# A bidirectional Hyena and gated-MLP block on one core: the second half's pairs in another order, and the DFT jobs spread over the first half of the output projection

## The chip, the cores and the metric

The kernel runs on one core of a Trainium2 chip. The metric is device time in microseconds (us) for one execution.

## What is computed

The block works on x of 2048 tokens by 1024 channels in float32. One input projection to 7168 channels feeds two branches, whose outputs go through one output projection. Cut to what matters here:

```python
proj = rms_norm(x, pre_norm_w) @ w_in
hy_in, hy_gate, sg_u, sg_v, sg_gate = split(proj, [3*D, 4*D, 5*D, 6*D])
x0, x1, v = split(short_conv_centred(hy_in, conv_w, conv_b), 3)
k = hyena_filter(...)                                   # a 4096-long filter per channel
y_a = x0 * long_conv_bidir(v * x1, k, skip) * silu(hy_gate)          # branch A, by DFT
vn = layer_norm_per_head(sg_v)
mixed = einsum('hpq,bnqhd->bnphd', sgu_w, vn) + sgu_b                # 128x128 per head
y_b = sg_u * mixed * silu(sg_gate)                                   # branch B
out = x + rms_norm(concat([y_a, y_b]) @ w_out, post_norm_w)
```

## The kernel before

**Pairs.** Each large product is done by a two by two scheme with seven products in place of eight, over *pairs* of 128-channel blocks. `self.order` is a list of 72 pairs (half, kind, index, and two weight blocks). Half 0 and half 1 are the two halves of the tokens. Kinds: U (x1 and v, whose product goes into the long convolution), G (x0 and branch A's gate), V (two heads of the gating values), B (branch B's gate and sg_u), O (two output blocks). For O the numbers 0 and 1 name not tokens but input channels: O(0) multiplies branch A's channels, O(1) branch B's, and the two partial sums are added. A pair is 84 matmuls of 128x512: seven units of four blocks, each in three matmuls over high and low parts (L304, L305, L306). A stream of pairs sets the order: products 0 to 4 of a pair, then products 5 and 6 behind product 0 of the next.

**Factors.** The moving operands are seven tiles `x`, one for each unit. When half or channels change they are loaded again: `load_x` (L554) loads them and splits them into high and low parts (L558, L559). At the change to `"w0"` (`turn`) the next pair's weights may not be loaded before all background jobs are through, since they come from Y, which the jobs write. The weights of a pair (`wraw`, `ws`, `wu`) are prepared a pair ahead (L606 to L637); for the second half most come back from DRAM (L631).

**Taking results.** A class for each kind (`TakeG`, `TakeV`, `TakeB`, `TakeO`) reads the banks in four calls, c11, c22, c21, c12, the last two in the next pair. V starts `v_job`: for each head transposes (L980), statistics (L984, L985), square root (L987), scaling (L992), mixing matmuls (L997) and the last step on VectorE (L1000); for half 1 the result goes to DRAM as VM (L969). B of half 1 loads it as `vm` (L174), multiplies (L1005) and writes Y. The first O stage writes partial sums to PT (L236, L243); the second loads them (`o_load`), and `o_job` (L1129 to L1134) does the post-norm.

**Background jobs.** DFT work runs beside the pairs as generators. `background(jobs, rate)` sets how many start at a tick; a pair has 3.5 ticks. 32 forward jobs (`fft_job`, two channel halves of 16 jobs): load, DFT matmul (L1070), complex product with the filter on VectorE (L1073, L1077), second DFT matmul (L1082), write BY. 32 inverse jobs (`inv_job`): load BY, inverse DFT matmul (L1108), transpose (L1114), times XG from the G pairs (L1115), write Y (L1116). An inverse job needs all forward jobs of its channel half and the XG of its channels.

**Order.** A scheduler places the instructions of each engine; each engine then works in order, SP (which issues most transfers) too. Buffers are rings: all tiles made by `wide` share four in this stage (`nw_`), those by `f` share six (`nf`), `ws` has three. A tile taken from a ring waits until the oldest is free.

Of the kernel before, what the change touches and what calls it, by code (L numbers as in the profile page):

```python
# [125 lines left out]
class TakeU(Take):  # L126
# [4 lines left out]
    def c22(self, C, u3):  # L131
        self.rv = self.b.wide([128, 18, 64], "rv")
        self.b.add(self.rv[:, 9:17].rearrange("q j p -> q (j p)"), C, u3)
# [83 lines left out]
class TakeO(Take):  # L217
# [5 lines left out]
    def c22(self, C, u3):  # L223
        self.y[1] = self.b.wide([128, 1024], "y1")
        self.b.add(self.y[1][:, 512:], C, u3)
        if self.h:
            self.part = [self.b.o_load(2 * self.c + 1 - n) for n in range(2)][::-1]

    def c21(self, B):
        y = self.y[1][:, :512]  # L230
        if self.h:
            self.nc.vector.tensor_tensor(y, B, self.part[1][:, :512], op=ALU.add)
            self.b.go(self.b.o_job(2 * self.c + 1, self.y[1], self.part[1], 512))
        else:
            self.nc.scalar.copy(y, B)
            self.nc.sync.dma_start(self.b.PT[2 * self.c + 1], self.y[1])  # L236

    def c12(self, C, u2):
        self.b.add(self.y[0][:, 512:], C, u2)
        if self.h:  # L240
            self.b.go(self.b.o_job(2 * self.c, self.y[0], self.part[0], 0))
        else:
            self.nc.sync.dma_start(self.b.PT[2 * self.c], self.y[0])  # L243


class Body:
# [77 lines left out]
    def build(self):  # L324
        with ExitStack() as st:
            self.pp = st.enter_context(self.pool("pp", space=PSUM))
            self.dp = st.enter_context(self.pool("dp", space=DRAM))
            self.cp = st.enter_context(self.pool("cp"))
            dram = lambda n, s, dt=F32: self.dp.tile(s, dt, name=n)
            self.AU = dram("AU", [256, NJ, D])  # L330
            self.AK = dram("AK", [256, NJ, D])
            self.KF = dram("KF", [2, 32, 128, 512])
            self.BY = dram("BY", [256, NJ, D])
            self.XG = dram("XG", [NJ, 128, 8, 128])
            self.UG = dram("UG", [8, 128, D])
            self.VM = dram("VM", [8, 128, 8, 128])
            self.U0 = dram("U0", [8, 128, D])
            self.Y = dram("Y", [NJ, 128, 16, 128])
            self.WT = dram("WT", [2, 7, 128, 4, 512])
            self.PT = dram("PT", [NJ, 128, D])  # L340
            self.RB = dram("RB", [D])
            self.GD = dram("GD", [NJ, 128, 2, 128])
            self.XS = dram("XS", [7, 128, 4, 512])
            self.load_consts()
            self.xp = st.enter_context(self.pool("xp"))
            U = lambda h: [(h, "U", c, 8 + c, 16 + c) for c in range(8)]
            G = lambda h: [(h, "G", c, c, 24 + c) for c in range(8)]
            B = lambda h: [(h, "B", c, 48 + c, 32 + c) for c in range(8)]
            V = lambda h: [(h, "V", c, 40 + c, 41 + c) for c in range(0, 8, 2)]
            GV = lambda h: [p for n in range(4) for p in G(h)[2 * n:2 * n + 2] + V(h)[n:n + 1]]  # L350
            O = lambda r: [(r, "O", m, 2 * m, 2 * m + 1) for m in range(8)]
            self.order = B(0) + U(0) + GV(0) + U(1) + GV(1) + B(1) + O(0) + O(1)
            self.at, self.prev, self.to_spill = 0, None, []
            self.WS = {p[1:3]: dram(f"WS{p[1]}{p[2]}", [len(SPILL), 128, 2, 512]) for p in self.order[:28]}
            self.seen = set()
            self.wp = st.enter_context(self.pool("wp"))
            with self.pool("rp") as self.rp:
                with self.pool("xs") as xs:
                    self.x_phase(xs)
                with self.pool("sg") as self.fp:  # L360
                    self.nw_ = 3
                    with self.pool("mlp") as ml:
                        self.mlp(ml)
                    with self.pool("k1") as kp:
                        self.background(self.k1_jobs(kp), 1.4)
                        self.run(self.stream(8))
                        self.rest()
                with self.pool("fa") as self.fp:
                    self.nw_, self.nf = 4, 8
                    self.background(self.x_jobs(1), 0.25)  # L370
                    self.run(self.stream(8))
                    self.rest()
                self.nc.sync.dma_start(self.rc, self.RB.rearrange("(c q) -> q c", c=8))
                with self.pool("fd") as self.fp:
                    self.nw_, self.nf, self.nl = 5, 2, 3
                    self.background(self.kfft_jobs(), 0.85)
                    self.run(self.stream(12, 1))
                    self.rest()
                with self.pool("fb") as self.fp:
                    self.nw_, self.nf = 4, 3  # L380
                    self.f1 = self.fp.tile([128, 2, 2, 128], F32R, name="f1")
                    self.nc.gpsimd.dma_start(self.f1, self.i["c_f1"])
                    self.background(self.wo_jobs(), 0.32)
                    self.run(self.stream(8))
                    self.rest()
                with self.pool("fc") as self.fp:
                    self.nw_, self.nf, self.nl = 4, 6, 4
                    self.background(self.fft_jobs(), 1.0)
                    self.run(self.stream(20, "w0"))
                with self.pool("fo") as self.fp:  # L390
                    self.nw_ = 4
                    self.pw = self.fp.tile([128, D], F32, name="pw")
                    self.nc.scalar.dma_start(self.pw, self.i["post_norm_w"].partition_broadcast(128))
                    self.run(self.stream(8, "w1"))
                    self.run(self.stream(8))
                    self.drain()

# [541 lines left out]
    def g_job(self, h, c, r0, sg):  # L939
        nc = self.nc  # L940
        t = self.wide([128, 1024], "t")
        self.conv(t, r0, c, h)
        rc = self.rc[:, c:c + 1]
        if h == 0:
            nc.vector.tensor_scalar(self.gedge[:, c:c + 1], sg[:, 1023:1024], rc, None, op0=ALU.mult)
        yield
        nc.vector.scalar_tensor_tensor(sg, sg, rc, t, op0=ALU.mult, op1=ALU.mult)
        nc.sync.dma_start(self.XG[:, :, c, 64 * h:64 * h + 64].rearrange("j q p -> q j p"), sg.rearrange("q (j p) -> q j p", j=NJ))
        if h:
            e = self.edge[:, c, 0:1]  # L950
            nc.vector.tensor_tensor(e, self.fix[:, c:c + 1], self.gedge[:, c:c + 1], op=ALU.mult)
            nc.sync.dma_start(self.XG[NJ - 1, :, c, 63:64], e)


    def v_job(self, h, hd, vr):
# [82 lines left out]
    def fft_jobs(self):  # L1038
        self.back = [0, 0]
        for g in range(0, 32, 2):  # L1040
            yield self.fft_job(g, 0)
        v = self.inv_jobs()
        for g in range(0, 32, 2):
            yield self.fft_job(g, 1)
            if g > 6:
                yield next(v)
        for _ in range(4):
            yield next(v)
        yield iter(())
        yield from v  # L1050

    def product_tile(self, name):

# [42 lines left out]

    def inv_job(self, j, h):
        nc, g1 = self.nc, self.g1
        assert self.back[h] == 32
        cs = slice(h * 512, h * 512 + 512)  # L1100
        raw = self.two("raw")
        nc.sync.dma_start(raw, self.BY[:, j, cs].rearrange("(d r) c -> r d c", d=2))
        yield
        xg = self.product_tile("xg")
        nc.sync.dma_start(xg.rearrange("q (c p) -> q c p", c=4), self.XG[j, :, 4 * h:4 * h + 4])
        ps = self.bank("b")
        for d in range(2):
            nc.tensor.matmul(ps, g1[:, d], raw[:, d], start=d == 0, stop=d == 1)  # L1108
        y = self.f("y")
        nc.scalar.copy(y, ps)  # L1110
        yield
        ps = self.bank("a")
        for q in range(4):
            nc.tensor.transpose(ps[:, q * 128:q * 128 + 128], y[:, q * 128:q * 128 + 128], self.ident)  # L1114
        nc.vector.tensor_tensor(xg, ps, xg, op=ALU.mult)  # L1115
        nc.sync.dma_start(self.Y[j, :, 4 * h:4 * h + 4], xg.rearrange("q (c p) -> q c p", c=4))  # L1116
# [53 lines left out]
```

## Time and profile before

| what | us |
|---|---|
| median of 3 runs | 2086.94 |
| lowest, highest | 2083.53, 2091.46 |
| the profiled execution | 2081.43 |
| its span, first to last instruction | 2079.6 |
| TensorE busy in it | 1907.2 |
| VectorE busy | 1347.8 |
| ScalarE, GpSimd busy | 855.0, 446.3 |

Busy time is the union of an engine's instructions. PE is TensorE's matmuls, PEld its weight loads, DVE is VectorE, ACT ScalarE, POOL GpSimd, SP the engine that issues transfers. A 128x512 DFT matmul in float32 makes two records in the trace and one row in the order below. TensorE can stand as busy while it gains little: a matmul's end is modelled, so short waits hide in the matmuls themselves. For that reason the time per matmul slot is used beside the busy share. The mean granted clock of TensorE was 0.975.

### The profile page before, as it was taken

The numbers are of one execution on the slowest core, as the hardware profiler recorded it, in microseconds if no ns is written. First come the engines' busy times: TensorE is split into PE (matmuls) and PEld (weight loads), VectorE is DVE, ScalarE is ACT, GpSimd is POOL, SyncE is SP. The second block draws the span as 40 slices with busy tenths as digits, with TensorE's granted clock in tenths as the row PEclk, the third lists the DMA queues.
The fourth block names the chain that finished last, engine by engine and source line by source line (L and its number), as shares of the span: only waits on it lengthen the run. The fifth ranks groups of instructions, "written<-read, shape, count | busy, mean of one in ns | idle before, by whom it ended". The sixth has DMA issues, their size and how long they took to land. (4 is left out here: it accounts for less than half of the span.)

```text
span 2079.6 us, 23943 instructions
## 1 busy us (share of the span) xinstructions
PE 1907.2 (92%) x7832; PEld 1419.1 (68%) x7832; DVE 1347.8 (65%) x2070; ACT 855.0 (41%) x1538; POOL 446.3 (21%) x392
## 2 busy tenths in 40 slices
PE   4689999999999999888999999989999999999997
PEld 3465666777777766666777666656677777887776
DVE  6767878787655545655544888887773226436876
ACT  6344444565434443534444223322322224335443
POOL 3431322233222121111111101101011112323331
PEclk9899999999999999999999999989999999999999
DMA  8388777786779796897786888878978888536563
GB/s 265 110 265 268 238 261 253 227 274 230 247 258 297 259 315 208 327 274 236 256 276 194 294 271 265 282 237 274 302 244 307 282 269 282 194 102 243 192 212 132
DMA packets 330203, 515.89 MB, mean 248 GB/s; under 512 B 107451, under 2 KB 177339, under 8 KB 327359
## 3 DMA queue, kind: packets, MB, share of 16 engines
q1 hardware_dynamic: 263328, 439.58, 64.9%
q10 hardware_dynamic: 61856, 69.81, 9.8%
q0 software_dynamic: 4896, 4.98, 1.0%
q8 instruction: 62, 1.02, 0.2%
q14 instruction: 61, 0.50, 0.1%
HBM read 316.10 MB, written 204.48 MB: 250 GB/s over the span
## 5 line engine op out<-in xcount | busy, mean ns | idle before, releaser
L304 PE MATMUL proj<-x,wu 128*128 128x512 f32 x2016 | 834.9, 415 | 36.0 <-ACT sn L648 15.1
L305 PE MATMUL proj<-x,wu 128*128 128x512 f32 x2016 | 808.2, 401 | 10.6 <-DVE wu L637 8.8
L306 PE MATMUL proj<-x,wu 128*128 128x512 f32 x2016 | 806.6, 400 | 1.2 <-DVE x L559 0.6
L304 PEld LDWEIGHTS proj<-x,wu 128*128 128x128 f32 x2016 | 383.6, 190 | 146.2 <-issue 32.8
L637 POOL TENSOR_TENSOR wu<-wraw,wu 128x512 fp32r<-128x512 f32 x172 | 257.3, 1497 | 1038.1 <-ACT wu L635 855.5
L305 PEld LDWEIGHTS proj<-x,wu 128*128 128x128 f32 x2016 | 383.7, 190 | 113.3 <-issue 24.9
L306 PEld LDWEIGHTS proj<-x,wu 128*128 128x128 f32 x2016 | 383.2, 190 | 94.6 <-issue 12.7
L635 ACT CAST wu<-wraw 128x512 fp32r<-128x512 f32 x216 | 133.5, 619 | 281.6 <-PE proj L306 240.3
L637 DVE TENSOR_TENSOR wu<-ws,wu 128x512 fp32r<-128x512 f32 x176 | 129.7, 739 | 156.0 <-ACT wu L635 155.6
L635 ACT CAST wu<-ws 128x512 fp32r<-128x512 f32 x176 | 108.6, 620 | 220.3 <-PE proj L306 160.3
L648 ACT COPY sn<-proj 128x512 f32<-128x512 f32 x216 | 125.6, 581 | 108.4 <-PE proj L306 80.3
L614 POOL TENSOR_TENSOR ws<-wraw 128x512 f32<-128x512 f32 x44 | 79.0, 1795 | 174.5 <-DVE wu L637 111.7
L1073 DVE TENSOR_TENSOR pa<-b,k 64x512 f32<-64x512 f32 x128 | 87.4, 683 | 40.6 <-PE b L1070 29.8
L614 POOL TENSOR_TENSOR ws<-wraw,ws 128x512 f32<-128x512 f32 x44 | 59.5, 1353 | 223.4 <-DVE wu L637 210.1
L1073 DVE TENSOR_TENSOR pb<-b,k 64x512 f32<-64x512 f32 x128 | 88.8, 694 | 1.8
L614 DVE TENSOR_TENSOR ws<-wraw 128x512 f32<-128x512 f32 x44 | 39.6, 901 | 71.3 <-DMA wraw<-in_w_in_dram 39.2
L1082 PE MATMUL b<-pa,tb 128*128 128x512 f32 x128 | 71.7, 645 | 15.1 <-DVE pa L1077 5.5
L1084 ACT COPY ev<-b 128x512 f32<-128x512 f32 x64 | 37.4, 587 | 99.4 <-PE b L1082 88.8
L559 DVE TENSOR_TENSOR x<-x 128x1024 fp32r<-128x1024 f32 x42 | 56.3, 1381 | 19.2 <-ACT x L558 19.2
L1033 PE MATMUL b<-raw,tk 128*128 128x512 f32 x128 | 62.9, 612 | 5.5 <-issue 4.8
L862 PE MATMUL b<-s,ff 128*128 128x512 f32 x128 | 62.2, 603 | 4.4 <-ACT ev L864 2.9
L1070 PE MATMUL b<-raw,tu 128*128 128x512 f32 x128 | 63.2, 604 | 1.7 <-DMA raw<-AU 1.7
(170 smaller groups left out, 2230.5 us busy)
## 6 DMA issues: line engine op xcount, KB each, us to landing
wraw<-in_w_in_dram SPq DMA_DIRECT2D x84, 512.0 KB, 4.9
WSB<-wu SPq DMA_DIRECT2D x32, 512.0 KB, 4.8
dd<-in_c_dec_dram SPq DMA_DIRECT2D x32, 512.0 KB, 5.6
AK<-ev ACTq DMA_DIRECT2D x64, 256.0 KB, 4.5
WSU<-wu SPq DMA_DIRECT2D x32, 512.0 KB, 4.5
WSG<-wu SPq DMA_DIRECT2D x32, 512.0 KB, 5.0
raw<-AK SPq DMA_DIRECT2D x32, 512.0 KB, 6.9
KF<-ev ACTq DMA_DIRECT2D x32, 512.0 KB, 6.0
```

What stands on the lines that cost most here:

```text
L304: t.matmul(ps, sh, mh, start=first, stop=False, **kw)
L305: t.matmul(ps, sl, mh, start=False, stop=False, **kw)
L306: t.matmul(ps, sh, ml, start=False, stop=last, **kw)
L614: eng.tensor_tensor(t, x, y, op=op)
L635: nc.scalar.copy(w[:, 0], src[u])
L637: eng.tensor_tensor(w[:, 1], src[u], w[:, 0].bitcast(F32), op=ALU.subtract)
L648: self.nc.scalar.copy(s, ps)
L862: nc.tensor.matmul(ps, self.ff[:, d], s[d], start=True, stop=True)
L1033: nc.tensor.matmul(ps, tv[:, n], raw[:, n], start=True, stop=True)
L1070: nc.tensor.matmul(u, tv[0][:, n], raw[:, n], start=True, stop=True)
L1073: nc.vector.tensor_tensor(o, uu, kk, op=ALU.mult)
L1082: nc.tensor.matmul(ps, tv[1][:, n], prod[n], start=True, stop=True)
```

## The change

The second half's pairs stand in another order. Before: G and V mixed, then B, then O(0), then O(1). Now: V and B mixed, then G, then O(1), then O(0). The O pairs of branch B, which need no DFT, move into the DFT stage, so that it has 28 pairs where it had 20. The forward jobs start at 0.55 a tick where jobs started at 1.0; after them come two blank ticks, then the inverse jobs at 1.05, where before the inverse jobs of the first channel half were mixed with the forward jobs of the second. Partial sums are written by O(1) and added in O(0). `xg` comes from the `f` ring (six tiles) where it came from the `ws` ring (three).

```diff
@@ TakeO: c22, c21, c12
-        if self.h:
+        if not self.h:
...
@@ build
-            self.order = B(0) + U(0) + GV(0) + U(1) + GV(1) + B(1) + O(0) + O(1)
+            VB = [V(1)[0]]
+            for n in range(4):
+                VB += V(1)[n + 1:n + 2] + B(1)[2 * n:2 * n + 2]
+            self.order = B(0) + U(0) + GV(0) + U(1) + VB + G(1) + O(1) + O(0)
...
-                    self.background(self.fft_jobs(), 1.0)
-                    self.run(self.stream(20, "w0"))
+                    self.background(self.fft_jobs(), 0.55)
+                    self.run(self.stream(20, "w1"))
+                    self.run(self.stream(8, "w0"))
                 with self.pool("fo") as self.fp:
...
-                    self.run(self.stream(8, "w1"))
                     self.run(self.stream(8))
@@ g_job
             nc.sync.dma_start(self.XG[NJ - 1, :, c, 63:64], e)
+            self.gated_c = c + 1
@@ fft_jobs
-        v = self.inv_jobs()
         for g in range(0, 32, 2):
             yield self.fft_job(g, 1)
-            if g > 6:
-                yield next(v)
-        for _ in range(4):
-            yield next(v)
-        yield iter(())
-        yield from v
+        for _ in range(2):
+            yield iter(())
+        self.rate = 1.05
+        yield from self.inv_jobs()
@@ inv_job
-        assert self.back[h] == 32
+        assert self.back[h] == 32 and self.gated_c >= 4 * h + 4
...
-        xg = self.product_tile("xg")
+        xg = self.f("xg")
```

`VB` is V V B B V B B V B B B B. In the changed kernel the lines of the DFT jobs and of the V jobs stand one to four higher: L1070, L1082, L1108 and L1114 are L1071, L1083, L1109 and L1115, and L997 is L1001.

What moves, at three places. First TensorE behind the last mixing matmuls (`b<-sw,vn`) of the half's second V pair, before. `pa,tb` is the second forward DFT matmul, `raw,tu` the first, `raw,g` the inverse one, `ident,y` its transposes, `proj` the pairs' products:

```order
L997 MATMUL b<-sw,vn 128x128 x8
L1082 MATMUL b<-pa,tb 128x512 x2
L1108 MATMUL b<-raw,g_10785 128x512 x2
L1070 MATMUL b<-raw,tu 128x512
L1114 MATMUL a<-ident,y 128x128 x4
L1070 MATMUL b<-raw,tu 128x512
L1082 MATMUL b<-pa,tb 128x512 x2
L1108 MATMUL b<-raw,g_10785 128x512 x2
L1070 MATMUL b<-raw,tu 128x512
L1114 MATMUL a<-ident,y 128x128 x4
L1070 MATMUL b<-raw,tu 128x512
L304 MATMUL proj<-x_6780,wu 128x512
```

And behind those of the third V pair of the half now:

```order
L305 MATMUL proj<-x_6780,wu 128x512
L1001 MATMUL b<-sw,vn 128x128
L306 MATMUL proj<-x_6780,wu 128x512
L1001 MATMUL b<-sw,vn 128x128 x2
L304 MATMUL proj<-x_6859,wu 128x512
L1001 MATMUL b<-sw,vn 128x128
L305 MATMUL proj<-x_6859,wu 128x512
L306 MATMUL proj<-x_6859,wu 128x512
L1083 MATMUL b<-pa,tb 128x512 x2
L1071 MATMUL b<-raw,tu 128x512
L304 MATMUL proj<-x_6859,wu 128x512
L305 MATMUL proj<-x_6859,wu 128x512
```

The mixing matmuls, two jobs' forward matmuls and two inverse jobs stood together; now single mixing matmuls stand between projections, and one forward job's behind them.

Second VectorE at the scaling (`vn`) of the same two V pairs, before (`pa`, `pb` are the complex product):

```order
L652 TENSOR_TENSOR r0_10681<-proj_10806,sn_10801 128x512
L1077 SCALAR_TENSOR_TENSOR pa_10506<-pb_10507,sgn_171,pa_10506 128x512
L1073 TENSOR_TENSOR pa_10572<-b_10570,k_10518 64x512 x2
L1073 TENSOR_TENSOR pb_10573<-b_10570,k_10518 64x512 x2
L1073 TENSOR_TENSOR pa_10581<-b_10579,k_10518 64x512
L1077 SCALAR_TENSOR_TENSOR pa_10572<-pb_10573,sgn_171,pa_10572 128x512
L1073 TENSOR_TENSOR pa_10581<-b_10579,k_10518 64x512
L1073 TENSOR_TENSOR pb_10582<-b_10579,k_10518 64x512 x2
L992 TENSOR_SCALAR vn_10633<-a_10615,mv_10621,rs_10630 128x128
L1077 SCALAR_TENSOR_TENSOR pa_10581<-pb_10582,sgn_171,pa_10581 128x512
L992 TENSOR_SCALAR vn_10633<-a_10615,mv_10621,rs_10630 128x128 x3
L992 TENSOR_SCALAR vn_10663<-a_10645,mv_10651,rs_10660 128x128 x4
```

And now:

```order
L992 RECIPROCAL rs_10181<-rs_10181 128x4
L989 BN_AGGR mv_10202<-bs_10201 128x2 x2
L996 TENSOR_SCALAR vn_10184<-a_10166,mv_10172,rs_10181 128x128 x4
L992 RECIPROCAL rs_10211<-rs_10211 128x4
L655 TENSOR_TENSOR sg_10321<-proj_10308,sn_10103 128x512
L996 TENSOR_SCALAR vn_10214<-a_10196,mv_10202,rs_10211 128x128 x4
L1074 TENSOR_TENSOR pa_10222<-b_10220,k_10131 64x512 x2
L1074 TENSOR_TENSOR pb_10223<-b_10220,k_10131 64x512 x2
L1074 TENSOR_TENSOR pa_10231<-b_10229,k_10131 64x512
L1078 SCALAR_TENSOR_TENSOR pa_10222<-pb_10223,sgn_171,pa_10222 128x512
```

Complex products of forward jobs stood between the statistics and the scaling, and between the two halves of the scaling; now the statistics, the scaling of one head and that of the other follow each other, and the product comes behind.

Third SP where the `vm` of a B pair is loaded, before (the first B pair, behind the last V pair):

```order
L1102 DMA raw_12499<-BY_66 128x2x512
L608 DMA wraw_12477<-in_w_in_dram 128x512
L969 DMA VM_69<-v0_12014 128x1024
L631 DMA wu_12404<-WSB1_92 128x1024
L1116 DMA Y_71<-xg_12290 128x512
L174 DMA vm_12450<-VM_69 128x1024
L969 DMA VM_69<-v1_12093 128x1024
L631 DMA wu_12452<-WSB1_92 128x1024
```

And now (the first B pair, behind the first two V pairs):

```order
L973 DMA VM_69<-v0_9288 128x1024
L964 DMA bi_10161<-in_sgu_b_dram 128x128
L962 DMA sw_10189<-in_sgu_w_dram 128x128
L634 DMA wu_9704<-WSB1_92 128x1024
L174 DMA vm_9685<-VM_69 128x1024
L973 DMA VM_69<-v1_9358 128x1024
L1061 DMA tu_9727<-in_c_tv_dram 128x2x128
L1024 DMA raw_9788<-AU_63 128x2x512
L1064 DMA k_9790<-KF_65 128x2x512
L634 DMA wu_9709<-WSB1_92 128x1024
```

The load of `vm` stood three rows behind the write of a V pair's first head, among inverse jobs' transfers. Now it stands four rows behind such a write, and the loads of the next forward job (`tu`, `raw`, `k`) and of the next pair's last weights (`wu`) stand behind it.

More of the change, by code (lines that the diff above doesn't have):

```diff
@@ L230, in c21 @@
         y = self.y[1][:, :512]
-        if self.h:
+        if not self.h:
             self.nc.vector.tensor_tensor(y, B, self.part[1][:, :512], op=ALU.add)
@@ L239, in c12 @@
         self.b.add(self.y[0][:, 512:], C, u2)
-        if self.h:
+        if not self.h:
             self.b.go(self.b.o_job(2 * self.c, self.y[0], self.part[0], 0))
```

## The prediction

> **What bounds the kernel now.** I read the page's first part, then the stretches of time with each engine's busy time, then TensorE's groups in the stage that changes, then VectorE's groups there.
>
> ```profile
> span 2079.6 us, 23943 instructions
> PE 1907.2 (92%) x7832; PEld 1419.1 (68%) x7832; DVE 1347.8 (65%) x2070; ACT 855.0 (41%) x1538; POOL 446.3 (21%) x392
> ```
>
> TensorE is busy for 92% of the span, so no other engine is the limit; only time in which TensorE stands or crawls can be won. The stretches below are cut at pair boundaries from the start of the DFT stage (columns: length; busy time and instructions of PE, PEld, DVE, ACT, POOL; granted TensorE clock; share and rate of the DMA engines).
>
> ```profile
> 1141.00:1307.70 166.70, 159.18 (x592) 103.68 (x591) 145.20 (x242) 52.01 (x90) 21.79 (x19) 1.00 0.86 278
> 1307.70:1402.40 94.70, 84.63 (x300) 51.94 (x299) 78.66 (x148) 27.03 (x46) 8.43 (x7) 0.93 0.79 256
> 1402.40:1565.40 163.00, 161.53 (x671) 113.49 (x670) 120.08 (x251) 49.00 (x87) 19.73 (x17) 1.00 0.84 275
> 1565.40:1726.40 161.00, 161.00 (x671) 118.68 (x670) 44.37 (x64) 42.71 (x71) 23.05 (x18) 1.00 0.88 283
> 1726.40:1790.10 63.70, 60.32 (x258) 48.50 (x258) 45.10 (x50) 31.27 (x46) 21.28 (x12) 0.97 0.76 270
> 1790.10:1885.30 95.20, 95.20 (x422) 78.86 (x421) 34.25 (x50) 31.50 (x55) 25.87 (x21) 1.00 0.37 121
> 1885.30:1946.50 61.20, 57.69 (x253) 47.14 (x252) 50.42 (x54) 35.18 (x53) 20.85 (x13) 1.00 0.68 250
> 1946.50:2068.50 122.00, 116.21 (x505) 93.95 (x503) 90.38 (x111) 49.15 (x94) 31.91 (x22) 1.00 0.57 185
> 2068.50:2079.60 11.10, 0.00 (x0) 0.00 (x0) 6.02 (x8) 1.44 (x3) 0.00 (x0) 0.70 0.24 94
> ```
>
> The first three are twelve pairs, G and V of the second half with all forward DFT jobs and 11 inverse ones. Then come six B pairs with inverse jobs (PE 161.00 of 161.00 us), the change to branch A's output channels, five pairs of the output projection alone (95.20 of 95.20), the change to branch B's, six pairs with the post-norm, and the tail. Five pairs are 420 projection matmuls, so one takes 95.20/420 = 0.227 us when nothing is in the way. The chain of waits gives the two other slots:
>
> ```profile
> 1721.68 0.44 PE a L1114 x4
> 1722.11 1.72 PE b L1108 x4
> ```
>
> 0.43 us for one record of a 128x512 DFT matmul, 0.11 us for a 128-wide one. What the twelve pairs hold:
>
> ```profile
> L304 PE MATMUL proj<-x,wu 128*128 128x512 f32 x336 | 145.6, 433 | 0.0
> L305 PE MATMUL proj<-x,wu 128*128 128x512 f32 x336 | 139.9, 416 | 0.0
> L306 PE MATMUL proj<-x,wu 128*128 128x512 f32 x337 | 138.3, 411 | 0.0
> L1082 PE MATMUL b<-pa,tb 128*128 128x512 f32 x126 | 70.6, 646 | 15.1 <-DVE pa L1077 5.5 <-issue 4.9 <-DMA tb<-in_c_tv_dram 2.3
> L1070 PE MATMUL b<-raw,tu 128*128 128x512 f32 x128 | 63.2, 604 | 1.7 <-DMA raw<-AU 1.7
> L1108 PE MATMUL b<-raw,g 128*128 128x512 f32 x44 | 22.1, 627 | 0.0
> L997 PE MATMUL b<-sw,vn 128*128 128x128 f32 x128 | 19.7, 287 | 2.1 <-DVE vn L992 1.4 <-DVE pb L1073 0.6
> L980 PE MATMUL a<-ident,v 128*128 128x128 f32 x64 | 9.8, 275 | 0.0
> L1114 PE MATMUL a<-ident,y 128*128 128x128 f32 x44 | 6.7, 275 | 0.0
> L962 PE MATMUL a<-sw,ones 128*128 128x128 f32 x16 | 3.2, 280 | 0.2 <-DVE bi L963 0.2
> ```
>
> That is 1009 x 0.227 + (126 + 128 + 44) x 0.43 + (128 + 64 + 44 + 16) x 0.11 = 229.0 + 128.1 + 27.7 = 384.8 us of work in 424.4 us (1141.0 to 1565.4). So 39.6 us are lost there. The windows show 7.5 + 10.1 + 1.5 = 19.1 us of it as idle and 0.07 x 94.7 = 6.6 us as half clock, 25.7 together; the rest hides in modelled ends (the projection matmuls show 411 to 433 ns). The largest single part stands in the second stretch:
>
> ```profile
> 1388.34 2.05 PE L1082 MATMUL b<-pa,tb 128*128 128x512 f32 x2 [3.59 <-issue]
> 1392.49 2.04 PE L1082 MATMUL b<-pa,tb 128*128 128x512 f32 x2 [2.11 <-DVE pa L1077]
> ```
>
> Here 28 matmuls of mixing and DFT stand in one heap with no projection between them (the first fence of the order, ahead), and TensorE waits 3.6 and 2.1 us inside it, at 2.05 us for two records that take half that elsewhere: half clock.
>
> Why it waits is VectorE, 145.20 + 78.66 + 120.08 = 343.9 of 424.4 us busy, 81%, and more in the first stretch (87%):
>
> ```profile
> L1073 DVE TENSOR_TENSOR pb<-b,k 64x512 f32<-64x512 f32 x128 | 88.8, 694 | 1.8
> L1073 DVE TENSOR_TENSOR pa<-b,k 64x512 f32<-64x512 f32 x128 | 87.4, 683 | 40.6 <-PE b L1070 29.8 <-DMA k<-KF 8.0 <-ACT ev L1084 0.3
> L1077 DVE SCALAR_TENSOR_TENSOR pa<-pb,sgn,pa 128x512 f32<-128x512 f32 x64 | 54.0, 843 | 0.2
> L992 DVE TENSOR_SCALAR vn<-a,mv,rs 128x128 f32<-128x128 f32 x64 | 21.9, 403 | 0.2
> L984 DVE BATCH_NORM_STATS2 bs<-a 128x6 f32<-128x128 f32 x64 | 16.1, 275 | 2.5 <-PE a L980 2.5
> L1000 DVE SCALAR_TENSOR_TENSOR v<-b,nw,bi 128x512 f32<-128x512 f32 x16 | 11.8, 739 | 3.7 <-PE b L997 3.6
> L985 DVE BATCH_NORM_AGGREGATE mv<-bs 128x2 f32<-128x6 f32 x64 | 10.0, 164 | 0.0
> L1115 DVE TENSOR_TENSOR xg<-a,xg 128x512 f32<-128x512 f32 x11 | 7.5, 682 | 17.2 <-PE a L1114 17.2
> ```
>
> The first three rows are the complex product: (88.8 + 87.4 + 54.0)/32 = 7.2 us of VectorE for each forward job. A V pair costs (21.9 + 16.1 + 11.8 + 10.0)/4 = 15.0 us in its four largest groups. At 3.5 forward jobs a pair VectorE needs 25.2 us for them alone, beside 32 to 36 us of TensorE per pair.
>
> **The change, part by part.**
>
> *Same work.* No matmul, vector operation or transfer is added or removed; TensorE's 7832 instructions only move. So the sum is over lost time alone.
>
> *Forward jobs at 0.55 a tick.* A pair has 3.5 ticks, so 1.9 jobs a pair where 3.5 stood, and the 32 jobs with two blank ticks reach 34/0.55 = 62 ticks, 17.7 of the 20 pairs. VectorE's load for them falls to 1.9 x 7.2 = 13.9 us a pair beside 84 x 0.227 + 1.9 x 8 x 0.43 = 25.6 us of TensorE. The heap goes too: the new order has projections among the mixing matmuls and the DFT matmuls behind them (second fence). What a pair without V still loses is bounded below by nothing (the 161.00 of 161.00 row) and above by the first stretch, 7.5/5 = 1.5 us visible, scaled by 39.6/25.7 to 2.3. I take 1.0, nearer to the third stretch, 1.5/5 = 0.3 visible and 0.46 scaled. Eight pairs: 8.0 us. For the five G pairs that now carry one job each, 0.5: 2.5 us; they were full as B pairs, so this is a loss against before.
>
> *V pairs.* The chain of a V pair (transposes, statistics, square root, scaling, mixing matmul, twice per head) has fewer DFT matmuls to hide behind now. Such pairs of the first half, which run beside light DFT work, and the last V pair of the second half:
>
> ```profile
> 600.80:633.30 32.50, 30.51 (x145) 24.00 (x144) 21.28 (x72) 13.05 (x23) 4.88 (x4) 0.95 0.57 183
> 684.10:720.50 36.40, 33.83 (x153) 25.45 (x152) 23.65 (x73) 15.09 (x27) 5.34 (x5) 0.95 0.67 232
> 771.70:805.40 33.70, 30.70 (x146) 23.88 (x145) 20.02 (x69) 12.97 (x23) 5.13 (x4) 0.95 0.44 155
> 857.40:896.20 38.80, 29.46 (x135) 23.72 (x135) 30.21 (x75) 16.69 (x26) 5.21 (x6) 0.87 0.82 290
> 1531.10:1565.40 34.30, 34.14 (x163) 25.70 (x162) 29.79 (x83) 9.26 (x17) 3.88 (x3) 1.00 0.68 219
> ```
>
> Idle plus what the clock took: 2.0 + 1.6 = 3.6; 2.6 + 1.8 = 4.4; 3.0 + 1.7 = 4.7; 9.3 + 5.0 = 14.3; and 0.2 us for the last, which stood among DFT jobs. Those are the bounds of one V pair. The new V pairs resemble the first three, so I take their mean, 4.2: 4 x 4.2 = 16.8 us. The fourth stood at a change of pools; it is the far end of the range.
>
> The Trainium skill, "TensorE: Matmul & The Clock Gate", Part 1 on the HAM clock gate, says that the clock halves only after a whole idle window of about 3.4 us. The trace does not bear that out here: the first of these rows is at 0.95 with 2.0 us of idle in all. By the page's rule the 1.6 to 1.8 us of clock would not be paid in the first three, a V pair would cost 2.5, and the sum would be 6.8 us lower.
>
> *V and B next to each other.* B's `vm` tile now reads VM two pairs after it is written, and takes the buffer of the V tile that writes it. On SP the load of `vm` stands four rows behind the write, with the next forward job's loads behind it.
>
> ```profile
> VM<-v SPq DMA_DIRECT2D x8, 512.0 KB, 3.7
> vm<-VM SPq DMA_DIRECT2D x8, 512.0 KB, 7.1
> ```
>
> Write and read are 3.7 + 7.1 = 10.8 us. Behind the product with `vm` on VectorE wait the adds of the next pair and the next DFT products. Bounds: nothing (it is loaded at the end of a pair and used in the next) and 10.8 us once. The first V and B are the only such tight neighbours, and most is covered by some 7 us of products; I take 1.0.
>
> *Inverse jobs under the output projection.* 32 jobs at 1.05 a tick end after 30.5 ticks, pair 26.4 of 28. In the five undisturbed output pairs VectorE works 34.25/5 = 6.9 us of 19.0; 3.7 inverse jobs add 3.7 x 0.68 = 2.5. TensorE gets 3.7 x (4 x 0.43 + 4 x 0.11) = 8.0 us more work, which leaves the B pairs. Bounds: nothing, as in the B pairs with the same 3.7 jobs, and 5.8/6 = 1.0 us a pair as under the post-norm, 8 us. I take nothing, since the B row holds the same jobs.
>
> *The changes of factors.* Loading and splitting the seven x tiles lost 3.4 + 0.03 x 63.7 = 5.3 us at the first change and 3.5 at the second. Both stay. The first now meets G's convolution and inverse jobs, the last one the inverse transposes, which stand two products (24 x 0.227 = 5.4 us) later than before, but B's last three transfers are gone from SP there. I take no difference; the bounds are 8.8 us either way (all gone, or doubled).
>
> *xg in another ring, the flag, PT:* the xg tile moves from a ring of three to one of six, no instruction more; PT is written in the pairs that wrote it before and read in the last eight. Post-norm and tail stay at 5.8 and 11.1 us. Each is nothing, hidden under the same pairs as before.
>
> Sum: lost before 39.6; after 8.0 + 2.5 + 16.8 + 1.0 = 28.3; gain 11.3 us. The profiled execution took 2081.4 us (span 2079.6 and 1.8 around it), 5.5 below the median of the three runs, 2086.9. So 2070.1 for one like it, and 2075.6 against the median, 0.54% faster. About 0.5% (10.4 us) is what a measurement of this kernel can tell from no change.
>
> **Rivals.**
>
> *The V pairs hide.* If the spread matmuls cover the mixing chains as they did the last V pair (0.2 us), with 0.46 us for the eight and 0.2 for the five others, 0.8 + 3.7 + 1.0 = 5.5 are lost, gain 34: 2053; with V at 1.5, 2058. For it: that row. Against it: it had heaped DFT jobs beside it, the new V pairs have one or two.
>
> *The loss moves to the factor changes and the projection.* Gain of 11.3, but 5 to 9 us come back where inverse jobs now meet the preparation of output weights: 2081 to 2085, no change that can be told. For it: the chain at the first change passes SP and VectorE. Against it: the DMA engines were busy for 0.76 at that change and 0.37 in the projection, so there is room for the jobs' transfers.
>
> *Slower: V pairs in a bare stream.* Two V pairs follow each other at once, with all four `wide` buffers held, and B must take them back. If each V pair costs what the worst of the first half did, 4 x 14.3 + 8.0 + 2.5 + 1.0 = 68.7 us are lost, 29 more than now: 2116. It decides at (39.6 - 11.5)/4 = 7.0 us a V pair; above 9.6 the kernel is slower by over 0.5%. For it: that row had the same buffers to wait for. Against it: three of four stayed under 5.
>
> **How the numbers follow.** Chances: the forecast 0.52 (its own range 2067 to 2082), V pairs hidden 0.14, loss moved 0.24, slower 0.10. The forecast's part below 2076.5 is some 0.6 of it: faster 0.14 + 0.31 = 0.45, slower 0.10, within 0.5% the other 0.45. The range 2058 to 2091 leaves out about half of the hidden case and nearly all of the slower one, and takes in the doubled factor changes (2075.6 + 8.8 = 2084).
>
> **What would show it.** Right: no heap, and the stretch of twelve V and B pairs shorter than 424 us by more than the 31 us of DFT work and 24 us of inverse work that leave it (9 x 8 x 0.43 and 11 x 2.16); the eight output pairs with inverse jobs full; VectorE near 76% in the V and B pairs, (343.9 - 9 x 7.2 - 11 x 0.68)/(424 - 55 - 11). Wrong: `L1001 <- DVE` waits of over 7 us a V pair, granted clock under 0.95 there, or idle time over 10 us at a change of factors.

## The result, and the profile after

The changed kernel takes 2074.3 us in the median of 5 runs (2066.24 to 2080.18); the kernel before, on the same chip, 2085.82 (2082.41 to 2091.46). The ratio is 0.9942, with a 95% interval of 0.992 to 0.9965: some 12 us or 0.58% faster. The forecast was 2075.6. The profiled execution took 2075.84 us, span 2074.1. Three runs that took far longer than the others of their kernel (2251.2 us in the fifth experiment below, 2400.17 us in the second, 6693.6 us of the kernel before) are left out of all times and ratios; the first was the profiled one, so that kernel was profiled again.

The page's busy times, in the form that the prediction shows of before:

```profile
PE 1904.6 (92%) x7832; PEld 1421.4 (69%) x7832; DVE 1341.6 (65%) x2070; ACT 850.1 (41%) x1536; POOL 442.6 (21%) x392
```

TensorE has as many instructions as before (x7832), and its busy time is 2.6 us less. The stretches of time, with the columns as before (length; busy time and instructions of PE, PEld, DVE, ACT, POOL; granted TensorE clock; share and rate of the DMA engines), cut at the new places: twelve pairs from the first V pair's chain on (three rows), five G pairs, the last of the G pairs, the change to branch B's factors, five output pairs with inverse jobs, the change to branch A's, six pairs with the post-norm, the tail.

```profile
1146.70:1296.30 149.60, 145.59 (x639) 106.49 (x638) 118.21 (x287) 41.94 (x72) 20.24 (x15) 1.00 0.78 253
1296.30:1357.50 61.20, 57.92 (x216) 39.13 (x215) 45.62 (x65) 15.80 (x26) 8.64 (x6) 1.00 0.88 290
1357.50:1499.30 141.80, 138.58 (x553) 98.58 (x552) 103.23 (x189) 42.16 (x70) 21.02 (x16) 1.00 0.83 266
1499.30:1629.00 129.70, 127.81 (x489) 90.78 (x489) 90.21 (x126) 41.59 (x78) 20.14 (x20) 1.00 0.83 256
1629.00:1678.00 49.00, 48.92 (x205) 36.81 (x204) 25.44 (x30) 21.21 (x36) 9.90 (x8) 1.00 0.85 276
1678.00:1736.40 58.40, 55.44 (x225) 39.19 (x224) 34.09 (x40) 25.57 (x41) 12.57 (x9) 1.00 0.84 272
1736.40:1873.20 136.80, 136.80 (x574) 100.81 (x573) 46.30 (x69) 42.58 (x74) 26.50 (x21) 1.00 0.65 216
1873.20:1941.00 67.80, 63.56 (x265) 50.96 (x264) 50.80 (x56) 35.64 (x54) 19.77 (x12) 0.95 0.79 286
1941.00:2063.00 122.00, 116.20 (x505) 93.96 (x503) 90.59 (x111) 49.12 (x94) 31.90 (x22) 1.00 0.57 185
2063.00:2074.10 11.10, 0.00 (x0) 0.00 (x0) 6.00 (x8) 1.44 (x3) 0.00 (x0) 0.72 0.24 94
```

Read the first three rows against the first three of before. The twelve pairs last 352.6 us where they lasted 424.4. The granted clock is 1.00 in all three; the stretch with the heap had 0.93. VectorE is busy for 118.21 + 45.62 + 103.23 = 267.06 of 352.6 us, 76% (81% before). TensorE idles 4.0 + 3.3 + 3.2 = 10.5 us where it idled 19.1. The five output pairs that now carry inverse jobs are full: 136.80 of 136.80 us. The change to branch A's factors is the one place that looks worse: 67.80 us at a clock of 0.95.

TensorE's groups in the twelve pairs show what it still waits for (busy time, mean ns of one, then idle time just before and what ended it):

```profile
L1083 PE MATMUL b<-pa,tb 128*128 128x512 f32 x92 | 48.5, 614 | 9.0 <-DVE pa L1078 3.5 <-DMA tb<-in_c_tv_dram 3.1 <-PE proj L306 0.9
L1071 PE MATMUL b<-raw,tu 128*128 128x512 f32 x96 | 47.1, 600 | 1.5 <-DMA raw<-AU 1.5
L1001 PE MATMUL b<-sw,vn 128*128 128x128 f32 x128 | 18.9, 275 | 0.0
L984 PE MATMUL a<-ident,v 128*128 128x128 f32 x64 | 9.7, 274 | 0.0
```

The mixing matmuls of the V pairs (L1001) wait for nothing, where `b<-sw,vn` waited 2.1 us; what idle time there is stands before the two forward DFT matmuls.

**Lost time by stretch.** As in the prediction, lost time is the length of a stretch less its slots (0.227 us for a projection matmul, 0.43 for a record of a 128x512 DFT matmul, 0.11 for a 128-wide one), here worked out pair by pair for two executions of each kernel. Small negative values come from rounded slots. "Part" is the time from the first of the twelve pairs (1141.0 before, 1146.7 after) to the end of the last matmul.

| us lost in | before | before, once more | after | after, once more |
|---|---|---|---|---|
| the twelve pairs | 40.7 | 39.8 | 20.7 | 22.9 |
| the next five pairs | 0.9 | 0.9 | 5.2 | 5.2 |
| four pairs to the first change | 6.1 | 5.1 | 5.8 | 6.8 |
| five output pairs | -0.2 | -0.2 | 0.6 | 0.6 |
| three pairs at the second change | 4.0 | 7.6 | 8.1 | 8.1 |
| six pairs with the post-norm | 7.6 | 7.5 | 7.5 | 7.5 |
| part, us | 927.5 | 929.1 | 916.3 | 919.7 |

The part is shorter by 927.5 - 916.3 = 11.2 us in the first pair of executions and by 929.1 - 919.7 = 9.4 in the second. In front of the part the instructions are the same in both kernels, and yet their lost time differs by up to some 14 us between the profiled executions: a single execution cannot tell a difference of 10 us in the whole time, so the experiments are read by the part, and by the ratio of their timed runs.

### The profile page after: what moved, and what is told of

It reads as the page before. It is cut to its first block, busy times and chain, and to the rows that moved or that the text cites. A ratio compares the mean times of both kernels' runs of the same rounds, so it can differ in the third digit from the quotient of the medians.

```text
span 2074.1 us, 23969 instructions
## 1 busy us (share of the span) xinstructions
PE 1904.6 (92%) x7832; PEld 1421.4 (69%) x7832; DVE 1341.6 (65%) x2070; ACT 850.1 (41%) x1536; POOL 442.6 (21%) x392
## 5 line engine op out<-in xcount | busy, mean ns | idle before, releaser
L305 PE MATMUL proj<-x,wu 128*128 128x512 f32 x2016 | 806.8, 400 | 12.0 <-DVE wu L640 10.2
L304 PEld LDWEIGHTS proj<-x,wu 128*128 128x128 f32 x2016 | 384.8, 191 | 152.5 <-issue 39.6
L617 DVE TENSOR_TENSOR ws<-wraw 128x512 f32<-128x512 f32 x44 | 39.8, 905 | 68.8 <-DMA wraw<-in_w_in_dram 43.2
L1083 PE MATMUL b<-pa,tb 128*128 128x512 f32 x128 | 67.7, 614 | 10.9 <-DVE pa L1078 4.6
L655 DVE TENSOR_TENSOR r<-proj,sn 128x512 f32<-128x512 f32 x64 | 43.9, 686 | 42.4 <-PE proj L306 41.9
```

What stands on the lines that cost most here:

```text
L304: t.matmul(ps, sh, mh, start=first, stop=False, **kw)
L305: t.matmul(ps, sl, mh, start=False, stop=False, **kw)
L617: eng.tensor_tensor(t, x, y, op=op)
L1083: nc.tensor.matmul(ps, tv[1][:, n], prod[n], start=True, stop=True)
```

## The experiments

Three theories stood at the start. Theory 1: the gain is from the density, since forward jobs at one a tick load VectorE more than a V pair can take. Theory 2: it is from taking the inverse jobs out from among the forward ones, since the heap held both. Theory 3: it is from the order of the pairs.

**1. The changed kernel with the forward jobs at one a tick.** The blank ticks make the inverse jobs start where they start in the changed kernel.

```diff
-                    self.background(self.fft_jobs(), 0.55)
+                    self.background(self.fft_jobs(), 1.0)
...
-        for _ in range(2):
+        for _ in range(30):
             yield iter(())
```

> The changed kernel with one thing undone: forward DFT jobs start at 1.0 a tick as before, not 0.55; 30 blank ticks behind them in place of 2 hold the inverse jobs at their place. Measured on the part from the first pair with forward jobs to the last matmul (927.5 us before, 916.3 in the changed kernel). Theory 1 (the gain is the lower density of forward jobs on VectorE): the twelve V and B pairs lose 30 to 40 us again in place of 21, the five G pairs behind them under 1 in place of 5, the part takes 922 to 931, ratio to before 0.997 to 1.001. Theory 2 (the gain is that no inverse job is mixed among forward jobs, so no heap): 913 to 919, ratio 0.992 to 0.996. Theory 3 (the gain is the new order of pairs): the same as theory 2.

Measured: 2099.73 us, 1.0069 (1.0047 to 1.0092) of before; part 937.6 us. The twelve pairs lose 47.3 us, the five behind them nothing. The windows of this kernel, two pairs with mixing matmuls and then the whole stretch of forward jobs:

```profile
1326.20:1368.30 42.10, 38.02 (x149) 26.14 (x148) 36.76 (x77) 9.98 (x17) 3.85 (x3) 0.92 0.74 240
1438.00:1479.20 41.20, 37.72 (x150) 26.33 (x149) 36.81 (x78) 11.94 (x18) 3.85 (x3) 0.92 0.82 260
1143.10:1512.30 369.20, 345.08 (x1303) 225.77 (x1302) 313.76 (x607) 102.32 (x169) 41.25 (x30) 0.98 0.84 273
```

In the two pairs the clock is 0.92, which takes 0.08 x 42.1 = 3.4 and 0.08 x 41.2 = 3.3 us, and TensorE stands 4.1 and 3.5 us. Two waits in the whole stretch that the changed kernel does not have:

```profile
PE b L1001 <- DVE vn L996: 6.0, 2, 3.5
PE proj L304 <- DVE rs L992: 3.2, 2, 1.6
```

The mixing matmuls wait 6.0 us for VectorE's scaling, 3.5 at once; in the changed kernel this wait is not there. With the density alone put back, all of the gain is gone and more: theory 1 holds in direction, and the order of pairs and the unmixed jobs are worth nothing without it. Its sizes missed: 30 to 40 us lost and a part of 922 to 931 were expected. By pairs, the three of this stretch without a V chain lose 1.9 to 2.9 us each, the seven with a piece of one 3.6 to 8.4.

**2. The kernel before with its inverse jobs behind all forward jobs.**

```diff
-        v = self.inv_jobs()
         for g in range(0, 32, 2):
             yield self.fft_job(g, 1)
-            if g > 6:
-                yield next(v)
-        for _ in range(4):
-            yield next(v)
         yield iter(())
-        yield from v
+        yield from self.inv_jobs()
```

> The kernel before with one thing done: inverse jobs all behind the forward jobs, not mixed with those of the second channel half; pairs and rate 1.0 as before. Theory 1 (density): the pairs with forward jobs still lose about 3 us each, ten of them 31, so the part falls from 927.5 to 917 to 923, ratio 0.995 to 0.999. Theory 2 (heap of mixed jobs): the heap of the second V pair (16.7 us) goes, others fall too: 908 to 915, ratio 0.987 to 0.993. Theory 3 (order of pairs): 925 to 929.

Measured: 2091.92 us in eleven runs, 1.0039 (1.0021 to 1.0057); part 935.6, the twelve pairs lose 48.8 us. That is outside what each of the three theories expected (917 to 923, 908 to 915, 925 to 929): the part grew. The heaps stay, at the second and third V pair:

```profile
1344.60:1397.50 52.90, 43.86 (x159) 27.54 (x159) 45.55 (x85) 12.91 (x22) 4.26 (x4) 0.90 0.71 227
1465.50:1515.90 50.40, 45.02 (x174) 28.65 (x173) 37.89 (x78) 15.27 (x26) 3.97 (x4) 0.90 0.76 248
```

52.9 and 50.4 us, 15.5 and 10.2 of them lost, at 0.90, with no inverse job in the first. Theory 2 falls: a heap is forward jobs and a V chain. The mixing even helped before: 8 us less are lost with it in the same twelve pairs (40.7 and 39.8). An inverse job takes a start that would go to a forward one, which fits theory 1, but was not tried by itself.

**3. The changed kernel with G and V first, then B, as before; the last two G pairs behind B.**

```diff
-            self.order = ... + U(1) + VB + G(1) + O(1) + O(0)
+            self.order = ... + U(1) + [p for p in GV(1) if p not in G(1)[6:]] + B(1) + G(1)[6:] + O(1) + O(0)
```

> The changed kernel with the pairs of the second half nearly in the old order: G and V mixed, then B, the last two G pairs at the end (Y of branch B must be written two pairs before the output projection reads it); rates and output stages as changed. Theory 1 (density) and theory 2 (no mixing): the part stays at 913 to 920, ratio 0.992 to 0.997. Theory 3 (order of pairs): 923 to 929, ratio 0.998 to 1.001.

Measured: 2080.53 us, 0.9983 (0.9967 to 0.9999); part 919.2. The twelve pairs lose 21.4 us and the next five 5.9, as after (20.7 and 5.2). Theory 3 falls for the DFT stage: with 0.55 a tick the old order loses no more. The part is as long as in the second execution of the changed kernel (919.7), with the first change of factors worse (9.9 us lost against 5.8 and 6.8) and the second better (5.5 against 8.1). The part came out as theories 1 and 2 expected, the ratio above their 0.992 to 0.997: it is 0.4% worse than the changed kernel's, more than the part says; what stands for the rest is not settled.

**4. The changed kernel with `xg` in the ring of three again.**

```diff
-        xg = self.f("xg")
+        xg = self.product_tile("xg")
```

> The changed kernel with xg back in the ring of three that the preparation of the output weights shares. The prediction counted this edit as nothing: the part stays at 914 to 919. Rival: the ring holds up the preparation in the eight output pairs with inverse jobs, 1 to 2 us a pair: 924 to 933.

Measured: 2094.21 us, 1.005 (1.0034 to 1.0066); part 938.6, 19 to 22 us more than after, and more than the rival expected (924 to 933). Most of it stands in the output pairs: 12.1 us are lost in the five that were full, 11.3 and 10.9 at the two changes. Those five pairs, and who waits for whom in them (TensorE, VectorE and SP's queue):

```profile
1739.80:1888.10 148.30, 141.00 (x573) 100.31 (x573) 51.14 (x69) 41.77 (x74) 26.94 (x20) 0.99 0.63 202
...
PE a L1115 <- DVE xg L1116: 7.1, 10, 2.2
...
DVE xg L1116 <- DMA xg<-XG: 19.8, 10, 6.7
...
SPq L1106 <- DVE wu L640: 21.6, 5, 7.0
SPq L1106 <- DMA Y<-xg: 19.2, 9, 3.1
```

A load of `xg` (L1106) needs a tile of the ring that also holds the output weights, and SP waits there until VectorE has split such weights (`wu`, 21.6 us) or an earlier `xg` has been written to Y (19.2 us); in the changed kernel it waits 0.2 us at this load in the same five pairs. Then VectorE waits for `xg` (19.8), and TensorE's transposes for VectorE's product (7.1). Without this small part of the change, inverse jobs under the output projection cost more than the whole change gains.

**5. The bare V chain.** The changed kernel with 28 blank ticks ahead of the forward jobs, which then run at one a tick: the V pairs have no DFT beside them.

```diff
-                    self.background(self.fft_jobs(), 0.55)
+                    self.background(self.fft_jobs(), 1.0)
...
         self.back = [0, 0]
+        for _ in range(28):
+            yield iter(())
```

> The changed kernel with no forward job under the first V pairs: 28 blank ticks first, then forward jobs at 1.0, inverse jobs where they were. This shows the V pairs bare, and forward jobs at full density with no V pair under them. The price that the prediction took for a V pair: 4.2 us each, 4.2 x 4 = 17 us in the first eight pairs; the rival's price 14.3 each, 57 us; if they hide, under 6. The nine or ten pairs with 3.5 forward jobs and no V: about 3 us each if VectorE's load from the jobs alone costs, 25 to 35; under 10 if only V and jobs together cost.

> The kernel after with the forward transform held back by 28 blank rounds and then run at one job a tick, so that the first V pairs run with no transform beside them; the profile of the first look at it was taken at a clock of 0.80 and cannot be read in us. Theory of the prediction (a V pair hides its chain behind its matmuls when nothing else is beside it, at most 7.0 us a pair when it does not): the V pairs without a forward job lose under 2 us each, and the forward jobs, which run at one a tick in the pairs behind them, lose 1.4 to 1.6 us a job, as they did in the kernel before and with one job a tick, 45 to 51 us for the 32. Rival (the bare V chain is what costs, 14.3 us a pair, the prediction's rival on the slower side): at least 7 us of lost time in each bare V pair.

Measured: 2077.67 us in nine runs, 0.9977 (0.9961 to 0.9993); in the second profiled execution, one run of 2085.08 us against 2084.11 of the kernel before, the part takes 920.4 us. Its windows: the first, second and third V pair's chain, the fourth with the first job beside it, and then the forward jobs at one a tick.

```profile
1151.80:1177.00 25.20, 25.20 (x138) 21.31 (x137) 15.69 (x61) 5.30 (x11) 3.83 (x3) 1.00 0.79 254
1177.00:1202.40 25.40, 25.36 (x138) 21.34 (x137) 15.76 (x61) 8.16 (x14) 3.83 (x3) 1.00 0.52 159
1240.40:1265.60 25.20, 25.20 (x138) 21.44 (x138) 15.32 (x61) 9.78 (x15) 3.85 (x3) 1.00 0.44 146
1303.60:1331.50 27.90, 27.90 (x144) 22.46 (x144) 21.35 (x70) 9.82 (x16) 3.85 (x3) 1.00 0.48 163
1331.50:1627.40 295.90, 285.41 (x987) 180.46 (x986) 251.58 (x360) 85.71 (x153) 38.60 (x33) 0.99 0.90 289
```

TensorE is busy 25.20 of 25.20 us in the first: 84 x 0.227 + 52 x 0.11 = 24.8 us are its slots. The four lose 0.4, 0.6, 0.4 and 0.6 us. The rival (14.3 us a pair) falls, and so does the prediction's own price of 4.2: a bare V pair hides. In the nine pairs of the last row, without a V chain, 28.8 jobs lose 25.9 us, which is in the 25 to 35 that the first expectation gave for VectorE's load from the jobs alone; it is 0.9 a job, where the second expected 1.4 to 1.6. So one job a tick costs little more a job than 0.55 (0.8 to 0.9, below), as long as no V chain stands beside it. In the first experiment the 32 jobs at 0.9 would lose 28.8 us; the other 18.5 of its 47.3 us, 4.6 a V pair, are there only when a V chain and dense forward jobs share VectorE (6.0 + 3.2 us of waits and 6.7 of clock are what the rows above show of it). Theory 1 has to be put more narrowly: it is density in V pairs.

**6. How the loss grows: 0.7 a tick.**

```diff
-                    self.background(self.fft_jobs(), 0.55)
+                    self.background(self.fft_jobs(), 0.7)
...
-        for _ in range(2):
+        for _ in range(12):
```

> The changed kernel with forward jobs at 0.7 a tick in place of 0.55 and 12 blank ticks in place of 2, the inverse jobs at their place. The seventeen pairs that hold forward jobs at 0.55 lose 25.9 us, and 47.2 at 1.0. Theory of a loss that grows with density: 30 to 37, part 920 to 928. Theory of a threshold (VectorE hides all until its load passes TensorE's, which it does near 0.9): 24 to 28, part 914 to 919.

Measured: 2073.25 us, 0.9959 (0.9942 to 0.9976); part 915.2. The twelve pairs and the next five lose 27.6 + 1.5 = 29.1 us. Per forward job, over all its pairs, that is 0.91 us; 0.81 and 0.88 at 0.55 (25.9/32 and 28.1/32), 1.48 at one a tick with the V pairs in it (47.3/32). The part falls in what the threshold expects, and the loss between the two; a fair reading, with one execution at 0.7, is a slow growth up to 0.7 and a steep one between 0.7 and 1.0 where V chains stand among the jobs.

**7 and 8. Later stretches.** The inverse jobs faster, so that they end before the second change of factors; and the forward jobs slower with faster inverse ones.

```diff
-        self.rate = 1.05
+        self.rate = 1.3
```

> The changed kernel with the inverse jobs at 1.3 a tick, not 1.05, so that the last ends some two pairs before the second change of factors and not in the last pair before it. Parts are measured from the first pair with forward jobs to the last matmul (916.3 us in the changed kernel). Theory A (the three pairs at the second change lose 8.1 us, where the same place lost 4.0 to 6.0 before, because the last inverse transposes and their transfers stand on SP ahead of the factor loads): they lose 3 to 5.5, the part takes 911 to 915, ratio to before 0.989 to 0.994. Theory B (they lose it because the post-norm's loads begin at once behind the change): still 7 to 9, the part 914 to 919.

```diff
-                    self.background(self.fft_jobs(), 0.55)
+                    self.background(self.fft_jobs(), 0.5)
...
-        self.rate = 1.05
+        self.rate = 1.25
```

> The changed kernel with forward jobs at 0.5 and inverse jobs at 1.25 a tick: the first inverse jobs come behind the first change of factors, the last still in the last pair before the second. Growth with density: the pairs with forward jobs lose 22 to 26 in place of 25.9; the first change of factors 4 to 5.5 (5.2 in the pair of it); the second change stays at 7 to 9 by theory A and by theory B. Part 911 to 917, ratio 0.990 to 0.995.

Measured: 0.9944 (0.9925 to 0.9963), 2071.1 us, part 916.4; and 0.9938 (0.9923 to 0.9953), 2069.55 us, part 909.9. The second change loses 3.9 and 3.4 us where the changed kernel loses 8.1. In experiment 7 theory A expected that, but a part of 911 to 915, which missed. In experiment 8 neither theory expected it; the pairs with forward jobs (some 24.5 us) and the first change (4.7) came out as expected, and the part below it. But experiment 6, with its inverse jobs as in the changed kernel, loses 4.0 there too. So it is not shown that the last inverse jobs cost anything at that change. The second of the two has the shortest part of all, and by its timed runs it can't be told from the changed kernel (the intervals overlap almost wholly).

**9 and 10. Both kernels a second time.** No edit.

> The kernel after with no edit, for a second profiled execution. If the 8.05 us lost in the three output pairs of the second change of factors, at a clock of 0.93, belong to the kernel, they come again at 7 to 9 us; if they belong to that one execution, 3.4 to 5.0 us, as in four of the experiments, and the changed part (first V pair to the end of the matmuls) comes out at 911 to 914 us instead of 916.3. The part in front, whose instructions are those of the kernel before, lost 178.7 to 188.0 us over the kernels looked at so far and should fall in that range.

> The kernel before with no edit, for a second profiled execution. If the heap is a property of the kernel before, one pair of the gate and value pairs again loses more than 10 us, the twelve pairs lose 37 to 50 us together, and the changed part is 925 to 937 us; if the 16.7 us of one pair belonged to one execution, the twelve lose under 30 us and the part is under 917 us, and the reading of the change falls with it.

Measured: 2076.39 and 2079.53 us, one run each. The heap is the kernel before's own: the second stretch has it again, 15.3 us lost in its one pair (16.7 the first time), and the twelve lose 39.8, with a part of 929.1 us, as expected of a heap that belongs to the kernel. At the second change the changed kernel loses 8.1 us again, so this did not belong to one execution; its part came out at 919.7. But the kernel before loses 7.6 us there this time, at the same clock. The heap's stretch, its pair, and the second change in the kernel before; then the second change in the changed kernel:

```profile
1304.70:1398.10 93.40, 82.22 (x300) 50.77 (x299) 78.60 (x148) 27.04 (x46) 8.42 (x7) 0.96 0.81 260
1341.30:1398.10 56.80, 46.99 (x174) 28.79 (x174) 47.27 (x88) 15.10 (x26) 4.24 (x4) 0.94 0.78 244
1879.90:1944.60 64.70, 60.89 (x253) 49.39 (x252) 50.69 (x54) 35.16 (x53) 20.97 (x13) 0.95 0.65 238
```

```profile
1872.30:1940.20 67.90, 63.57 (x266) 50.97 (x265) 50.20 (x56) 35.52 (x54) 19.61 (x12) 0.95 0.80 285
```

## Why the prediction was right, and where its terms were off

The time came within 1.3 us of the forecast, and the part within 0.1 and 1.9 us of the gain. That is better than the terms were, and in part luck: two of them were wrong in opposite directions, as shown below.

*The lost time before, 39.6 us:* 40.7 and 39.8 by pairs. It was a real loss of the kernel, heap included, and experiments 1 and 2 show where it is from: V chains and forward jobs at one a tick, both waiting for VectorE. The heap's pair alone loses 16.7 and 15.3 us of it, more than the whole gain.

*V pairs, 4 x 4.2 = 16.8:* mis-sized. Alone the four lose 0.4 to 0.6 us each; in the changed kernel, with their forward jobs, 3.6, 1.3, 0.1 and 1.2, so 6.2 together. The rows of the first half that were taken as nearest, 3.6 to 4.7 a pair, pay for something that the new ones don't have. Each holds one wait, of the chain's transposes for the `v` that VectorE takes from the product, and the fall of the clock that the prediction added to it:

```profile
PE a L980 <- DVE v L652: 2.0, 1, 2.0
PE a L980 <- DVE v L652: 2.6, 1, 2.6
PE a L980 <- DVE v L652: 3.0, 1, 3.0
```

In the second half the same transposes wait for nothing (L980 in the prediction's rows, L984 above); why is not shown. The row that was set aside, the last V pair of the half at 0.2, was the near one. The reason given for setting it aside, that it stood among heaped DFT jobs, is the wrong way round: a V chain needs no DFT matmul to hide behind, the 84 projection matmuls are enough. The rival "slower" with its 14.3 us falls with that.

*The other pairs, 8 x 1.0 = 8.0:* mis-sized the other way. Together with V and the 1.0 for VM the twelve were to lose 25.8; they lose 20.7 and 22.9. With 2.0 of it for the V chains (0.4 + 0.6 + 0.4 + 0.6, as alone), some 19 to 21 us are left for 23.5 forward jobs, 0.8 to 0.9 a job, where 8.0 over the 15.2 jobs of eight pairs made 0.5. So at 0.55 a tick the loss goes with the number of forward jobs rather than with that of pairs or V chains.

*Five G pairs, 2.5:* 5.2 both times. Here the number of jobs was wrong as well: 8.5 forward jobs run there, not one a pair (the prediction's own 1.9 jobs a pair would have given nine or ten); at 0.6 a job that is 5.2.

The two errors have opposite signs: 28.3 us forecast for all of these, 25.9 and 28.1 measured. The rival "V pairs hide" had the V term right and still gave 2053 to 2058, because it let the other pairs hide too.

*VM round trip, 1.0:* TensorE has no wait for it, and VectorE waits 1.3 us for `vm` in all:

```profile
L1009 DVE TENSOR_TENSOR ug<-ug,vm 128x512 f32<-128x512 f32 x16 | 12.1, 757 | 1.6 <-DMA vm<-VM 1.3
```

*Inverse jobs under the output projection, 0:* right, 0.6 us in five pairs, and 136.80 of 136.80. But the sum did not see on what it rests: the step "`xg` in another ring" was put at nothing, and experiment 4 prices its absence at 19 to 22 us. The edit itself adds no time, as forecast; but it is the condition on which the inverse jobs hide, and the prediction should have named and priced it.

*The changes of factors, no difference:* at the first 5.8 and 6.8 against 6.1 and 5.1, right. At the second 8.1 and 8.1 against 4.0 and 7.6: 4 us worse by the first two executions and 0.5 by the second two. The same two waits stand there in both kernels, for the weights (`wu`) and for ScalarE's copy of the product before (`sn`). First before, then after, then before once more:

```profile
PE proj L305 <- DVE wu L637: 1.9, 1, 1.9
PE proj L304 <- ACT sn L648: 1.6, 1, 1.6
```

```profile
PE proj L305 <- DVE wu L640: 1.8, 1, 1.8
PE proj L304 <- ACT sn L651: 2.4, 1, 2.4
```

```profile
PE proj L304 <- ACT sn L648: 2.0, 1, 2.0
PE proj L305 <- DVE wu L637: 1.9, 1, 1.9
```

The waits are within 0.8 us of each other; what differs is whether the clock falls behind them (1.00 in the first, 0.95 in the other two). The wait for `sn` is the longer one in the changed kernel, and whether that makes the fall of the clock more frequent is open: two executions of each can't tell.

*The Trainium skill, "TensorE: Matmul & The Clock Gate", Part 1:* by its rule, which asks for a whole idle window of about 3.4 us, a V pair would have cost 2.5 and the sum would have been 6.8 us lower. The V pairs did cost less, but not for that reason: in the changed kernel they idle for 2.8 us in all four together, at a clock of 1.00. Where the trace does show a fall of the clock, at the second change, the longest single wait is 1.8 to 2.4 us, so the condition is again not borne out. The length agrees better with the window that the Trainium skill gives: the last pair of the change in the changed kernel runs at 0.92,

```profile
1918.30:1941.00 22.70, 20.90 (x85) 16.79 (x84) 17.68 (x22) 10.27 (x19) 8.40 (x5) 0.92 0.69 240
```

so 0.08 x 22.7 = 1.8 us are lost, which is some 3.6 us at half speed.

*What would show it:* six of the eight output pairs with inverse jobs are full, and the other two stand at the changes of factors (5.0 and 4.4 us lost); no pair of the twelve loses more than 4.0 us, so there is no heap; the stretch is shorter by 71.8 us, more than the 55 of work that was to leave it; VectorE stands at 76% as forecast; none of the three signs of a wrong forecast came, since the waits before the mixing matmuls are nil, the clock there 1.00, and the idle time at the changes 3.0 and 4.2 us.

Left open: the 0.4% of experiment 3 that its part does not show, the clock at the second change, and what the 0.8 to 0.9 us that each forward job still loses consists of beyond the waits for `pa`, `tb` and `raw` shown above.

## What to carry to other kernels

When background work and a latency chain share a helper engine, look at what they ask of it in the same pair, not at its average: VectorE was 85% busy in the stretches of forward jobs of both the first experiment (313.76 of 369.20 us) and the fifth (251.58 of 295.90), yet the loss per job was 1.5 us in the one, where V chains stood among the jobs, and 0.9 in the other. Either thinning the jobs or keeping them out of those pairs takes the difference away; 0.8 to 0.9 us a job stay. And price an edit that looks free by undoing it alone: a ring of six tiles in place of three was worth more here (19 to 22 us of the part) than the new order of the pairs (at most some 3 us of the part, 0.4% by the timed runs).

## What the runs showed that was not expected

In the kernel before the clock fell to 0.95 over the second change behind two waits of 2.0 and 1.9 us in one execution, and stayed at 1.00 behind two of 1.6 and 1.9 us in another; the change lost 7.6 us in the one and 4.0 in the other. And the time that the same instructions in front of the changed part lost differed by up to some 14 us from one execution to another, as much as the whole change is worth.
